# Lower-part score products over 128 rows instead of 64, in a two-block transformer kernel

## Chip, cores and metric

The kernel runs on one core of one Trainium2 chip. The metric is device time in microseconds (us) of one execution: the median of the runs shown. Engines in the profile: PE (TensorE matmul), PEld (its weight load), DVE (VectorE), ACT (ScalarE), POOL (GpSimd), SP (SyncE, which issues most DMAs).

## What is computed

Two transformer blocks of two layers each, on 256 tokens of width 1024, in f32. The first block mixes three attentions: a linear recurrence (RWKV-7), a dilated attention and a latent attention (MLA), each with 4 heads. The second mixes stick-breaking attention, a block-sparse one (which is plain causal at this length) and attention on a memory of 256 rows. Each layer of the first block ends with a gated feed-forward network. The scores that the change touches are these (cut):

```python
# latent attention: 128 columns "nope" and 64 rotated columns per head
s = (jnp.einsum('bqhd,bkhd->bhqk', qn, k_nope)
     + jnp.einsum('bqhd,bkd->bhqk', qr, k_rope)) * scale
# dilated, block-sparse and memory attention: heads of 64
s = jnp.einsum('...qhd,...khd->...hqk', q, k) * 64 ** -0.5
# recurrence, per head of 64, token after token
sa = jnp.einsum('bhvk,bhk->bhv', state, kk_t)
state = state * w_t - sa * b_t + v_t * k_t
y = jnp.einsum('bhvk,bhk->bhv', state, r_t)
```

The recurrence is computed in two halves of 128 tokens, in matrix form: its "scores" are products of (kk, r) with (b, k), masked to the past, and the inverse of a triangular matrix.

## The kernel before, in words

All operations are first recorded, in an order in which they could run one by one, by class `Plan` (line 208 on). `Plan.order` (430) then sorts them with a table of costs (`cost`, 303), gives each tile a place, and `issue` (546) emits the sorted list: every engine's order is fixed by it. A tile of fp32r type lies in an arena of `SPLIT` = 11264 columns (34), f32 tiles in another, and each waits for a free stretch of columns (`_find`, 338). `hold` (289) lets an operation wait for another one.

Matrices of weights come as pieces (`load`, 832): a DMA into `raw`, a cast to fp32r (`whi`, by ACT or DVE) and a subtraction for the rest (`wlo`, by DVE or POOL). `multiply` (863) makes three fp32r products per tile, upper with upper, upper with lower, lower with upper, all with 128 rows. This stream of weights goes on while attention runs, as far as the data allow.

Scores of heads of 64 that need the precision of f32 go through `stacked` (918). Two heads lie on the 128 partitions, one on 0 to 63 (q = 0), the other on 64 to 127 (q = 1). For each q, a tile `hi[q]` has the upper parts of that head on its own 64 partitions; on the other 64 it has, by a DMA of the POOL queue, the same again (queries, `twice`) or the lower parts (keys). So one product over 128 rows gives upper·upper + upper·lower. The third term, lower parts of the queries with upper parts of the keys, is a second product over the own 64 rows alone (`krl[rs]`, `dql[rs]`, `bql[rs]`, `ms["ql"][rs]`), into the same bank. Such pairs of products are in `rwkv` (1171, 8 pairs for each half of the tokens), `dilated` (1430, 4 pairs, second half alone), `moba` (1653, 6 pairs, second half alone) and `memory` (1669, 4 pairs per half): per layer 16 + 4 in the first block and 6 + 8 in the second, 68 in all.

In `mla` (1377) a head's scores are an f32 product over the 128 "nope" rows and an f32 product over 64 rotated rows, per block of 128 keys: 4 pairs for the first half of the tokens and 8 for the second, 24 in the two layers. An f32 product leaves two MATMUL records in the trace, an fp32r one leaves one.

Of the kernel before, what the change touches and what calls it, by code (L numbers as in the profile page):

```python
# [112 lines left out]
class View:  # L113
    """A slice of a tile that has no address yet: how to take it, and which part it covers."""
# [51 lines left out]
    @staticmethod  # L166
    def meet(r, q):
        """Whether two regions may share an element; a comb is (distance of its teeth, from, to)."""
        if r[0] > q[1] or q[0] > r[1] or r[2] > q[3] or q[2] > r[3]:
            return False  # L170
        a, b = r[4], q[4]
        return a is None or b is None or a[0] != b[0] or (a[1] < b[2] and b[1] < a[2])
# [8 lines left out]
class Tile(View):  # L181
    """ring: of how many slots, taken in turn, the tile takes one; 0: a place of its own in the arena."""
# [27 lines left out]
class Plan:  # L210
    """Takes the operations of the kernel in an order in which they could run one by one, gives
    the tiles their places, and issues the operations in an order in which no engine waits for
    one while it could run another."""
# [75 lines left out]
    def hold(self, o, d):  # L289
        """Let o, the last one recorded, wait for d."""  # L290
        if d is not None and d not in o.deps:
            o.deps[d] = True
            o.need += 1
            d.succ.append(o)
# [37 lines left out]
    def _kind(self, t):  # L332
        """Which arena the tile t lies in, and what it takes of it."""
# [4 lines left out]
    def _find(self, t, strict):  # L338
        """(time from which it is free, where) for the tile t, or None if it has to wait."""
# [73 lines left out]
    def flush(self, sizes, window):  # L413
        """Order and issue all that is recorded."""
# [15 lines left out]
    def order(self, sizes, window, strict, tiles):  # L430
# [23 lines left out]
        # the clock of TensorE is halved when less than a third of a window of 3.4 us was busy  # L454
# [113 lines left out]
class Piece:  # L568
    """A part of a weight matrix: ks k tiles of w columns, and its place among the k tiles of the activations."""
# [6 lines left out]
class Chunk:  # L576
    """Products of the activations lhs() with some columns of a weight matrix.

    rows: (bank, columns of a piece, how many) -> [token, column], for each half of the tokens
    cols: (bank, which half of it, first of 128 columns) -> [column, token], both halves at once  # L580
    """
# [9 lines left out]
def kernel(ctx: ExitStack, tc: tile.TileContext, ins, out):  # L591
# [66 lines left out]
    # cos and sin of the angles, both halves: [pos, 16 | pos, 64 | token index, 16]  # L658
# [31 lines left out]
    def rope(t, h, lo, n, heads):  # L690
        """Half-split rotation, in place, of t: [P, heads, 2, n]."""
# [9 lines left out]
    def rsqrt(v, n, most=None, soon=False):  # L701
        """1 / sqrt(v) of [P, n], v kept."""
# [38 lines left out]
    def rstd_of(src, soon=False):  # L741
        """1 / rms of the rows of src: [P, D]."""
# [9 lines left out]
    def across(r, dst):  # L752
        """The column r [P, 1] as a row dst [P, 128] on every partition."""
# [8 lines left out]
    def parts(n, tag):  # L762
        """Transposed activations of both halves, in two parts: [channel, half, k tile, token]."""
        return tuple(T([P, 2, n, P], tag + s, F32R) for s in ("h", "l"))

    def fill(dst, h, src, j, g):
        """Columns j*512..+512 of the rows src, transposed, times g [P, k tile], split."""
# [17 lines left out]
    def cut(loads, kts, w):  # L785
        """Pieces of at most two k tiles and 1024 columns in all."""
# [17 lines left out]
    def row_chunk(w, ca, cb, lhs, done, pre=None):  # L804
        """Columns ca..cb, as rows of tokens."""
# [3 lines left out]
    def col_chunk(w, spans, lhs, done, pre=None):  # L809
        """The columns of the spans, 128 to a block, as columns of tokens: done(block, [P, 256])."""  # L810
# [8 lines left out]
    def out_chunk(w, ks, banks, lhs, done, n):  # L819
        """Rows of a [K, 1024] matrix, one k tile to a piece: ks are (k tile of w, of the activations)."""  # L820
# [7 lines left out]
    def meanwhile(n, f):  # L828
        """Record f, loads above all, when n more pieces have come, to start when the last of them is split."""
        pending.append((count[0] + n, f))  # L830
# [32 lines left out]
    def multiply(h, chunk, pi):  # L863
        """The rows of half h of a piece, and with half 0 its columns."""
# [7 lines left out]
        def product(key, a, b, acc, pairs):  # L872
            """acc += of three products; the first in a bank clears it."""
# [29 lines left out]
    def run():  # L903
        """Record the stream: the second half of the tokens runs LAG pieces behind the first."""
# [13 lines left out]
    def stacked(dims, tag, twice, srcs):  # L918
        """srcs, (which part of [P, ...dims], what), heads of 64 by two, split for products over 64: [q]
        with the upper parts of the heads 2p + q on their own partitions, and on the other 64 the same  # L920
        again (twice) or the lower parts; and the lower parts of all."""
        hi = [T(dims, f"{tag}{q}", F32R) for q in range(2)]
        lo = T(dims, tag + "l", F32R)
        for part, src in srcs:
            for q in range(2):
                plan.either("copy", part(hi[q]), src)
            nc.vector.tensor_tensor(part(lo), src, part(hi[0]).bitcast(F32), op=OP.subtract)
        pat = "p a b c -> p (a b c)" if len(dims) == 4 else "p a b -> p (a b)"
        for q in range(2):
            own, other = slice(64 * q, 64 * q + 64), slice(64 - 64 * q, 128 - 64 * q)  # L930
# [22 lines left out]
    def flip(S, n, nkh):  # L953
        """[P q, n, nkh*128] -> [P keys, n, nkh, 128 q]."""
# [9 lines left out]
    def weigh(pts, vs, pairs, nkh):  # L964
        """Heads of 64, transposed, [2 x 64, pair, 128 q]: the values vs(kh, head) under the weights pts[head]."""
# [27 lines left out]
    # =====================  keys and values of the memory  =====================  # L993
# [841 lines left out]
```

## Time and profile before

| | us |
|---|---|
| median of the runs (1050.58, 1052.13, 1053.52) | 1052.13 |
| span of the profiled execution, first to last instruction | 1050.8 |
| PE busy in it | 1005.6 |
| DVE busy | 763.1 |
| ACT busy | 513.2 |
| POOL busy | 208.4 |

The profile is one execution. Busy time is a union: a matmul's record runs from its start to its modelled end, and the next one starts long before that, so PE looks busy even where matmuls follow slowly. How fast matmuls go is read from the distances between their starts. The granted TensorE clock is 1 (2.4 GHz) or 0.5 (1.2 GHz). All instructions have the same source line, so rows are told apart by operation, tile and shape; `128*128 128x256` is a matmul of 128 rows by 128 columns of weights with 256 moving columns.

### The profile page before, as it was taken

What the parts mean: (1) busy time and instruction counts of PE and PEld (TensorE: products, weight loads), DVE (VectorE), ACT (ScalarE), POOL (GpSimd) and SP (SyncE); (2) the same over time, 40 slices, a digit from 0 to 9 for tenths busy, and PEclk for the clock granted to TensorE, in tenths of its full rate; (3) what the DMA queues carried; (4) which work ended last, traced back from release to release, by engine and by line L of the source; (5) the groups of instructions that cost most, each with busy time, mean ns of one, the idle gap of its engine ahead of it and who ended that gap; (6) DMA issues with size and microseconds to landing.
All of it is one profiled execution on the core that took longest, in us unless ns stands there. A gap on an engine that the chain in (4) does not pass through costs nothing.

```text
span 1050.8 us, 20310 instructions
## 1 busy us (share of the span) xinstructions
PE 1005.6 (96%) x7473; PEld 889.7 (85%) x7473; DVE 763.1 (73%) x1796; ACT 513.2 (49%) x1232; POOL 208.4 (20%) x313
## 2 busy tenths in 40 slices
PE   7789999999999998999999999999989999999997
PEld 6677889799999987787777999999878988889886
DVE  6797667886676767976757876667687787766884
ACT  5475665443333344553543433333466466554673
POOL 3263021210100115351412101001132011220120
PEclk9999899999999999987979999999999999999999
DMA  6836115566565647552224565656454435465341
GB/s 208 250 100 214 45 53 162 156 184 200 170 207 170 197 118 217 145 145 82 70 73 141 181 210 166 210 169 200 126 136 131 142 111 186 137 157 146 111 161 41
DMA packets 108311, 158.39 MB, mean 151 GB/s; under 512 B 8433, under 2 KB 91571, under 8 KB 108211
## 3 DMA queue, kind: packets, MB, share of 16 engines
q1 hardware_dynamic: 105011, 151.97, 48.1%
q0 software_dynamic: 3200, 5.11, 2.2%
q8 instruction: 59, 0.97, 0.4%
q14 instruction: 41, 0.34, 0.1%
HBM read 148.74 MB, written 1.05 MB: 143 GB/s over the span
## 4 chain that ended last, share of the span: by engine, by line
PE 79%; DVE 13%; DMA 3%; issue 2%; ACT 2%; POOL 1%; SPq 0%; ACTq 0%; DVEq 0%; POOLq 0%
PE bank L565 79%; DVE plain L565 7%; DVE small L565 3%; DVE wlo L565 2%; DMA plain<-plain 1%; DVE split L565 1%; POOL small L565 1%; DMA raw<-in_w_in_dram 1%; ACT plain L565 1%; SPq L565 0%; DMA small<-in_positions_dram 0%; DVE whi L565 0%; DMA plain<-in_gains_dram 0%; ACT whi L565 0%; ACT plain L561 0%
## 5 line engine op out<-in xcount | busy, mean ns | idle before, releaser
L565 PE MATMUL bank<-whi,split 128*128 128x512 f32 (+4 forms) x1416 | 428.0, 371 | 4.1 <-DVE split L565 4.1
L565 ACT CAST whi<-raw 128x512 fp32r<-128x512 f32 (+4 forms) x412 | 219.2, 562 | 294.6 <-PE bank L565 217.1
L565 PE MATMUL bank<-split,whi 128*128 128x256 f32 x1904 | 353.9, 284 | 0.0
L565 DVE TENSOR_TENSOR wlo<-raw,whi 128x512 fp32r<-128x512 f32 (+4 forms) x489 | 296.4, 643 | 31.3 <-ACT whi L565 18.2
L565 PEld LDWEIGHTS bank<-split,whi 128*128 128x128 f32 x1904 | 299.8, 189 | 9.1 <-issue 2.3
L565 PEld LDWEIGHTS bank<-whi,split 128*128 128x128 f32 x1416 | 264.1, 193 | 36.5 <-DVE split L565 5.7
L565 PE MATMUL bank<-split,wlo 128*128 128x256 f32 x952 | 269.8, 283 | 0.0
L565 PE MATMUL bank<-wlo,split 128*128 128x512 f32 (+4 forms) x708 | 263.0, 372 | 2.7 <-DVE wlo L565 2.7
L565 POOL TENSOR_TENSOR wlo<-raw,whi 128x384 fp32r<-128x384 f32 (+3 forms) x107 | 131.4, 1241 | 656.8 <-DVE plain L565 235.5
L565 PE MATMUL bank<-plain 32*32 32x32 f32 (+7 forms) x2309 | 186.2, 251 | 24.3 <-DVE plain L565 9.3
L565 PEld LDWEIGHTS bank<-plain 32*32 32x32 f32 (+4 forms) x2309 | 141.8, 141 | 63.5 <-issue 20.5
L565 PEld LDWEIGHTS bank<-split,wlo 128*128 128x128 f32 x952 | 180.0, 189 | 1.2 <-issue 0.5
L565 DVE CAST whi<-raw 128x512 fp32r<-128x512 f32 (+4 forms) x184 | 72.6, 399 | 129.6 <-PE bank L565 114.0
L565 PEld LDWEIGHTS bank<-wlo,split 128*128 128x128 f32 x708 | 137.1, 194 | 18.1 <-DVE wlo L565 3.3
L565 ACT ACTIVATE plain<-plain 128x256 f32<-128x256 f32 (+4 forms) x155 | 71.7, 476 | 80.7 <-DVE plain L565 77.5
L565 DVE TENSOR_TENSOR plain<-bank,plain 128x256 f32<-128x256 f32 (+4 forms) x134 | 63.2, 492 | 29.7 <-PE bank L565 26.4
L565 ACT COPY plain<-bank 128x256 f32<-128x256 f32 (+6 forms) x129 | 50.3, 406 | 56.7 <-PE bank L565 55.2
L565 DVE TENSOR_TENSOR plain<-plain 128x256 f32<-128x256 f32 (+7 forms) x137 | 67.1, 505 | 6.9 <-DMA plain<-plain 2.8
L565 DVE TENSOR_TENSOR split<-plain,split 128x256 fp32r<-128x256 f32 (+2 forms) x94 | 61.8, 674 | 0.8 <-ACT split L565 0.3
L565 PE MATMUL bank<-split 128*128 128x256 f32 (+2 forms) x168 | 53.8, 377 | 0.0
L565 ACT CAST split<-plain 128x256 fp32r<-128x256 f32 (+2 forms) x100 | 47.6, 488 | 12.3 <-DVE plain L565 12.1
L565 POOL TENSOR_TENSOR small<-small 128x1 f32<-128x1 f32 (+2 forms) x98 | 28.0, 287 | 88.9 <-DVE small L565 68.5
(61 smaller groups left out, 521.9 us busy)
## 6 DMA issues: line engine op xcount, KB each, us to landing
raw<-in_w_in_dram SPq DMA_DIRECT2D x80, 384.0 KB, 3.5
raw<-in_ffn_w_gate_dram SPq DMA_DIRECT2D x88, 256.0 KB, 2.9
raw<-in_ffn_w_up_dram SPq DMA_DIRECT2D x88, 256.0 KB, 3.3
raw<-in_ffn_w_down_dram SPq DMA_DIRECT2D x44, 512.0 KB, 4.5
raw<-in_w_out_dram SPq DMA_DIRECT2D x32, 512.0 KB, 3.5
raw<-in_w_in_dram SPq DMA_DIRECT2D x24, 352.0 KB, 3.5
raw<-in_w_mem_kv_dram SPq DMA_DIRECT2D x8, 512.0 KB, 4.9
raw<-in_w_in_dram SPq DMA_DIRECT2D x16, 256.0 KB, 2.8
```

The source lines that it names most:

```text
L565: getattr(eng, name)(*args, **kw)
```

## The change

In `stacked` the lower parts of queries become two tiles `lo[q]`, one per q, which hold the head's lower parts on its own 64 partitions and zeros on the other 64. The second product of a pair then runs over all 128 rows. Per call with `twice` (10 in all: 4 in `rwkv`, 2 each in `dilated`, `moba`, `memory`) this is one tile more, two POOL memsets of 64 partitions (held until the source is written), and two DVE subtractions of 64 partitions in place of one of 128. In `mla` the transposed rotated queries go into two tiles with zeros likewise (two POOL memsets, two copies of 64x256 and one of 128x128 in place of one of 128x384), the rotated keys of both halves lie side by side, and one product takes both key blocks: in the second half 8 pairs with 128 columns become 4 pairs with 256. Docstrings and comments that the diff drops are left out here.

```diff
@@ stacked @@
         hi = [T(dims, f"{tag}{q}", F32R) for q in range(2)]
-        lo = T(dims, tag + "l", F32R)
+        pat = "p a b c -> p (a b c)" if len(dims) == 4 else "p a b -> p (a b)"
+        sides = [(slice(64 * q, 64 * q + 64), slice(64 - 64 * q, 128 - 64 * q)) for q in range(2)]
+        if twice:
+            begun = srcs[-1][1].tile.writes[-1][0]
+            lo = [T(dims, f"{tag}l{q}", F32R) for q in range(2)]
+            for q, (own, other) in enumerate(sides):
+                plan.hold(nc.gpsimd.memset(lo[q].rearrange(pat)[other, :].bitcast(F32), 0.0), begun)
+        else:
+            lo = T(dims, tag + "l", F32R)
         for part, src in srcs:
             for q in range(2):
                 plan.either("copy", part(hi[q]), src)
-            nc.vector.tensor_tensor(part(lo), src, part(hi[0]).bitcast(F32), op=OP.subtract)
-        pat = "p a b c -> p (a b c)" if len(dims) == 4 else "p a b -> p (a b)"
-        for q in range(2):
-            own, other = slice(64 * q, 64 * q + 64), slice(64 - 64 * q, 128 - 64 * q)
+            if twice:
+                for q, (own, other) in enumerate(sides):
+                    nc.vector.tensor_tensor(part(lo[q])[own], src[own], part(hi[q])[own].bitcast(F32), op=OP.subtract)
+            else:
+                nc.vector.tensor_tensor(part(lo), src, part(hi[0]).bitcast(F32), op=OP.subtract)
+        for q, (own, other) in enumerate(sides):
             nc.gpsimd.dma_start(hi[q].rearrange(pat)[other, :], (hi[q] if twice else lo).rearrange(pat)[own, :])
@@ rwkv @@
-                        nc.tensor.matmul(b[:, p * 256:(p + 1) * 256], bk[q][rs, p, j, :], krl[rs, p, :, :], start=False, stop=True, skip_group_check=True)
+                        nc.tensor.matmul(b[:, p * 256:(p + 1) * 256], bk[q][:, p, j, :], krl[q][:, p, :, :], start=False, stop=True, skip_group_check=True)
@@ mla @@
             rope(qr[h].rearrange("p a (b c) -> p a b c", b=2), h, 8, 32, 6)
+            begun = plan.ops[-1]
...
-            rT = lat["r", h] = T([P, 3, P], "qrT")
-            plan.either("copy", rT.rearrange("p a b -> p (a b)"), b[:, :384])
+            rT = [T([P, 2, P], f"qrT{q}") for q in range(2)]
+            for q in range(2):
+                own, other = slice(64 * q, 64 * q + 64), slice(64 - 64 * q, 128 - 64 * q)
+                plan.hold(nc.gpsimd.memset(rT[q].rearrange("p a b -> p (a b)")[other, :], 0.0), begun)
+                plan.either("copy", rT[q].rearrange("p a b -> p (a b)")[own, :], b[own, 0:256])
+            if h == 0:
+                lat["r"] = T([P, 256], "krT")
+            plan.either("copy", lat["r"][:, h * P:(h + 1) * P], b[:, 256:384])
...
-                    for kh in range(nkh):
-                        o = bv[:, p, kh * P:(kh + 1) * P]
-                        nc.tensor.matmul(o, lat["q"][:, hd, h * P:(h + 1) * P], lat["k"][:, hd, kh * P:(kh + 1) * P], start=True, stop=False)
-                        nc.tensor.matmul(o, rT[rs, p, :], lat["r", kh][rs, 2, :], start=False, stop=True)
+                    nc.tensor.matmul(bv[:, p, :], lat["q"][:, hd, h * P:(h + 1) * P], lat["k"][:, hd, 0:nk], start=True, stop=False)
+                    nc.tensor.matmul(bv[:, p, :], rT[q][:, p, :], lat["r"][:, 0:nk], start=False, stop=True)
@@ dilated (moba and memory alike) @@
-                nc.tensor.matmul(dst, dql[rs, p, :], dk[q][rs, p, :], start=False, stop=True, skip_group_check=True)
+                nc.tensor.matmul(dst, dql[q][:, p, :], dk[q][:, p, :], start=False, stop=True, skip_group_check=True)
```

## Rows read from the trace of the kernel before

**Rows 1.** Page, part 1: busy us, share of the span, instructions of each engine.
```profile
PE 1005.6 (96%) x7473; PEld 889.7 (85%) x7473; DVE 763.1 (73%) x1796; ACT 513.2 (49%) x1232; POOL 208.4 (20%) x313
```
**Rows 2.** Page, part 4: the chain that ended last, by engine.
```profile
PE 79%; DVE 13%; DMA 3%; issue 2%; ACT 2%; POOL 1%; SPq 0%; ACTq 0%; DVEq 0%; POOLq 0%
```
**Rows 3.** That chain in order of time: start us, us, engine, out, instructions.
```profile
88.21 3.14 DVE wlo L565 x4
...
92.05 73.03 PE bank L565 x950
...
474.27 22.67 PE bank L565 x378
...
795.85 104.60 PE bank L565 x739
...
934.40 106.64 PE bank L565 x760
```
**Rows 4.** Groups by form, whole span: count | busy us, mean ns | idle before.
```profile
L565 PE MATMUL bank<-split 64*128 64x256 f32 x68 | 27.1, 398 | 0.0
```
**Rows 5.** Timeline of PE, memory scores, second block: start us, us, instruction, count.
```profile
854.89 2.57 PE L565 MATMUL bank<-split 128*128 128x256 f32 x8
857.39 0.39 PE L565 MATMUL bank<-split,wlo 128*128 128x256 f32 x1
```
**Rows 6.** Timeline of PE, stream of weights, feed-forward network.
```profile
300.01 0.28 PE L565 MATMUL bank<-split,wlo 128*128 128x256 f32 x1
...
300.37 0.28 PE L565 MATMUL bank<-split,wlo 128*128 128x256 f32 x1
```
**Rows 7.** Timeline of PE, end of the first block's attention, layer 2.
```profile
520.03 3.23 PE L565 MATMUL bank<-plain 128*128 128x128 f32 x27
...
523.01 1.92 PE L565 MATMUL bank<-split 128*128 128x256 f32 x6
...
526.54 0.59 PE L565 MATMUL bank<-whi,split 128*128 128x512 f32 x1 [1.60 <-DVE split L565]
```
**Rows 8.** Groups by form, PE, 145.8 to 149.5 us: latent scores, layer 1.
```profile
L565 PE MATMUL bank<-plain 64*128 64x128 f32 x12 | 2.4, 322 | 0.0
L565 PE MATMUL bank<-plain 128*128 128x128 f32 x10 | 2.1, 311 | 0.0
```
**Rows 9.** Timeline of PE, latent scores, layer 2, second half.
```profile
533.22 4.97 PE L565 MATMUL bank<-plain 64*128 64x64 f32 x15
538.12 0.79 PE L565 MATMUL bank<-wlo,split 128*128 128x512 f32 x1
```
**Rows 10.** Stretches: length, busy us of PE, PEld, DVE, ACT, POOL, granted clock, DMA.
```profile
95.50:100.10 4.60, 4.60 (x61) 2.85 (x46) 2.81 (x11) 1.43 (x2) 2.11 (x12) 1.00 0.51 185
100.20:110.30 10.10, 10.10 (x111) 8.81 (x114) 5.76 (x19) 4.53 (x9) 1.57 (x8) 0.50 0.12 29
...
462.00:468.70 6.70, 6.70 (x24) 5.97 (x24) 4.25 (x13) 1.96 (x5) 0.82 (x1) 0.50 0.56 177
...
479.10:492.60 13.50, 13.50 (x195) 10.68 (x195) 6.27 (x29) 3.40 (x14) 0.00 (x0) 0.50 0.01 4
...
526.90:540.40 13.50, 13.50 (x46) 9.85 (x46) 6.77 (x36) 5.81 (x20) 0.31 (x2) 0.50 0.30 106
```
**Rows 11.** Timeline of PE, stream products inside the third of these stretches.
```profile
483.10 0.41 PE L565 MATMUL bank<-split,wlo 128*128 128x256 f32 x1
483.31 0.52 PE L565 MATMUL bank<-whi,split 128*128 128x384 f32 x1
```
**Rows 12.** Groups by form, whole span: what waits for the products, and the nearest costs.
```profile
L565 DVE COPY_PREDICATED plain<-plain,bank 128x512 f32<-128x512 int32 x16 | 11.7, 733 | 9.1 <-PE bank L565 9.0
...
L565 DVE TENSOR_TENSOR split<-bank,split 128x512 fp32r<-128x512 f32 x16 | 10.8, 686 | 3.1 <-ACT split L565 3.0
...
L565 POOL MEMSET plain<- 128x512 f32 x16 | 8.0, 547 | 1.6 <-DVE plain L565 1.6
...
L565 DVE TENSOR_TENSOR plain<-bank,plain 64x512 f32<-64x512 f32 x2 | 1.4, 695 | 1.6 <-PE bank L565 1.6
```

More of the change, by code (lines that the diff above doesn't have):

```diff
@@ L1165, in rwkv @@
                 for q in range(2):
-                    rs = slice(64 * q, 64 * q + 64)
                     plan.hold(nc.gpsimd.memset(dst[q].rearrange("p a b c -> p (a b c)"), 0.0), begun)
@@ L1387, in mla @@
             for q in range(2):
-                rs = slice(64 * q, 64 * q + 64)
                 b = bank()
@@ L1654, in scores @@
                 nc.tensor.matmul(dst, bq[q][:, p, :], bk[q][:, p, :], start=True, stop=False, skip_group_check=True)
-                nc.tensor.matmul(dst, bql[rs, p, :], bk[q][rs, p, :], start=False, stop=True, skip_group_check=True)
+                nc.tensor.matmul(dst, bql[q][:, p, :], bk[q][:, p, :], start=False, stop=True, skip_group_check=True)
             groups = [(0, [0, 1, 2]), (1, [0, 1, 2])] if h == 0 else [(0, [0, 1]), (1, [0, 1]), (0, [2]), (1, [2])]
@@ L1671, in scores @@
                 nc.tensor.matmul(dst, ms["q"][q][:, p, hs], ms["k"][q][:, p, :], start=True, stop=False, skip_group_check=True)
-                nc.tensor.matmul(dst, ms["ql"][rs, p, hs], ms["k"][q][rs, p, :], start=False, stop=True, skip_group_check=True)
+                nc.tensor.matmul(dst, ms["ql"][q][:, p, hs], ms["k"][q][:, p, :], start=False, stop=True, skip_group_check=True)
             o = softmax_heads(
```

## The prediction

> **What bounds the kernel now.** I read the page's busy shares first: PE is busy for 1005.6 of 1050.8 us, DVE for 763.1, the others for half the span or less [rows 1]. Then the chain that ended last: 79% of it is PE, 13% DVE [rows 2]. In order of time the chain shows where: in layer 1 PE alone from 92.05 us on for 73.03 us, in layer 2 for 22.67 us from 474.27, and in the second block two unbroken stretches of over 100 us [rows 3]. The products that the change touches lie in or just ahead of those stretches. What stands between is DVE, as at 88.21 us, where four `wlo` subtractions release PE [rows 3]. So PE's time counts nearly one for one where the chain stays on PE, and hardly where DVE comes next.
>
> A busy PE says little of its pace, so I then read starts. The 68 products of 64 rows have records of 398 ns [rows 4], but the record has the latency in it. In the memory scores four pairs, eight products of 256 columns with 128 and 64 rows in turn, go from 854.89 to 857.39: 2.50 us, or 0.31 us a product, 0.625 a pair [rows 5]. The stream of weights issues products of the same 256 columns, all of 128 rows, accumulating into one bank as well: three from 300.01 to 300.37, 0.12 us each (0.119 over the five threes from there) [rows 6]. The alternating pair pays 0.39 us over two products of one form. Nothing waits for data in between; idle before the 64-row products is 0.0 [rows 4].
>
> The Trainium skill's page "TensorEngine Tiling (Array Packing)", section Key Properties, says that changing the tiling mode drains the TensorE; the trace agrees with 0.31 us against 0.12. The same page speaks against the change as well: its section When to Use Tiling wants row tiling where 64 or fewer rows are contracted, since two such tiles work side by side. By that, 68 products given up as halves would cost 34 times 0.12, some 4 us (an estimate by that page); here no two of them stand next to each other, each lies between products of 128 rows, so I put nothing for it.
>
> **The change part by part.**
>
> *Split pairs.* 68 pairs [rows 4], each 0.625 us now [rows 5], after it two products of one form, 0.24 us [rows 6]: 68 times 0.39 is 26.3 us off PE. Six of these pairs run at half clock, where the saving is larger; that is in the bounds of the clock below.
>
> *Latent scores.* An f32 product of 128 columns is two records, and 27 such in one form take 520.03 to 523.01, 0.110 us each [rows 7]. In layer 1, from 145.8 to 149.5, 22 records (12 of them of 64 rows, six products) take 3.7 us, 0.168 each [rows 8]: 22 times 0.058 is 1.3 us for six products, 0.21 each. In layer 2, second half, 15 records go from 533.22 to 538.12, 0.327 us each [rows 9], at half clock [rows 10], where a one-form product of 256 columns takes 0.21 [rows 11]; I take the same for a record there. That is 15 times 0.117, 1.8 us for three and a half products, 0.5 each. So 16 products at 0.21 and 8 at 0.5: 7.4 us. Bounds: 5 (first-half products whose neighbours stay in other forms save half) to 9.4 (24 times 0.39). Eight of the second half's 16 products per layer go, since one takes 256 columns; the columns are the same, so I put nothing for it, and half the weight loads, which overlap PE.
>
> *The clock.* Four stretches of 10.1, 6.7, 13.5 and 13.5 us run at 1.2 GHz, 43.8 us in all [rows 10]. Just ahead of the first, from 95.5 to 100.1, PE ran the recurrence's alternating pairs at full clock, 61 instructions with PEld busy for 2.85 of 4.6 us [rows 10]; the last starts after 1.60 us of idle [rows 7]. With the alternation gone PE does the same work in less time, and the clock may stay up. Upper bound: some 18 us of the 43.8 are changed products (6 pairs at about 1.0, 8 latent ones at 1.4), the other 26 would take 0.12 / 0.21 of that, 11 us less, and the changed ones 4 less: 15. Lower bound: another 10 us stretch falls, minus 4. I take plus 4, nearer to none, because the small products of the triangular inverse between, which fill the third stretch (195 instructions [rows 10]), stay as they are.
>
> *What is not cashed.* (1) Three dilated pairs of layer 2 run from 523.01 on and are followed by 1.60 us in which PE waits for DVE [rows 7]: minus 1.2. (2) The first half's eight recurrence pairs in either layer are followed by a DVE stretch, as at 88.21 [rows 3]. DVE itself waits for those products, 9.0 us in 16 masked copies [rows 12], so it gains too; I count half of 2 times 3.1 as lost: minus 3, bounds 0 to 6.
>
> *What is added.* (3) DVE: a subtraction of 64 partitions costs as much as one of 128, 695 against 686 ns for 512 columns [rows 12]. Ten calls make one more: four of 512 columns, 2.8 us, and six of 256 to 512, about 0.6 each, 3.5 us. In `mla` three copies replace one, at most 0.7 us [rows 12] four times. Nine us in all, on an engine that is 73% busy [rows 1]. What hides it is PE's own stream; where DVE is on the chain it is not hidden. I charge a quarter, minus 2 (bounds 0 to 9). (4) POOL: 28 memsets at 0.55 or less [rows 12], 15 us on an engine busy for 208.4 [rows 1]. Behind them in POOL's queue stand the rsqrt steps, its `wlo` parts, and the DMA that duplicates `hi`, for which the first product of each pair waits: at most 1.1 us per call, 11 us in all. They may start when the source is transposed, while the two copies of `hi` are still to be made, which that DMA needs anyway: minus 1 (0 to 11). (5) Places: at the recurrence of layer 2 the fp32r arena must hold `hT` (4096 columns), `cT` (1536) and ten tiles of 512 for both halves, 10752 of 11264; with twelve it would be 11776, so tiles of the second half wait until the first half's go free. The second half's products come more than 10 us later, so the wait is short: minus 1 (0 to 5). Other orders that the planner makes from this I can't price.
>
> *Sum.* 26.3 + 7.4 + 4 - 1.2 - 3 - 2 - 1 - 1 = 29.5 us. Against the profiled execution: 1050.8 - 29.5 = 1021.3; nothing outside its span is shown. The median lies 1.3 above that span, so 1022.6; I say 1022.
>
> **Rivals.**
>
> *DVE takes PE's place.* Where PE is faster in the first block, it waits for `wlo`, masked copies and casts instead. For it: DVE 73% busy, the stretch at 88.21 [rows 1, 3], and more DVE work. Against it: 73 us of chain on PE alone in layer 1 [rows 3], and DVE itself waits for the pairs [rows 12]. Then the second block's 28 pairs remain, 10.9 us, and a third of the first block's 15.5 + 7.4, 7.6, less 4 for the additions: 14.5, time 1037 (1034 to 1046).
>
> *The clock stays up.* All four stretches run at full clock: 11 more than in the sum, 1011, and with less lost to DVE down to 1002. For it: the first fall follows the alternation directly [rows 10]. Against it: the last follows idle [rows 7], and small products remain. By the Trainium skill, page "TensorE: Matmul & The Clock Gate", Part 1, the throttled state is the default and activity releases it, which would make this case; the trace bears it out in part, as one of the two falls shown follows idle, not sparse work.
>
> *The change doesn't do what it says.* The 0.31 us could come from two products in a row into the same bank, or from the same weights loaded twice, and not from 64 rows. Then pairs stay at 0.625 and only the additions remain: 1052 to 1058. Against it: the stream accumulates into one bank at 0.12 [rows 6].
>
> *Slower: the freed time of PE becomes idle, and the clock falls.* The place is the first block's attention, above all 92 to 165, where PE has no idle now. At half clock a product takes 0.21 instead of 0.12 [rows 6, 11], so each us there loses 0.43. From 78 us more at half clock on (33.7 / 0.43) the gain is gone; with 100 it would be 43 - 29.5, some 1065. Against it: half clock is 44 us of the whole now, and long stretches of the stream hold full clock.
>
> **Chances and range.** Forecast, 1010 to 1034: 0.67. DVE takes over: 0.17. Clock stays up, 1002 to 1010: 0.08. Not what it says: 0.05. Slower by the clock: 0.03. About 0.3%, some 3 us, is what a measurement of this kernel can tell from no change. The first three cases are all faster by more: 0.92. Of the fourth, 0.03 falls within 0.3% and 0.02 above, with 0.03 of the fifth: slower 0.05. The range 1003 to 1042 leaves out the last two cases (0.08), the upper third of the DVE case (0.05) and tails of some 0.04.
>
> **What would show it.** After the change the page should have no 64*128 form with `bank<-split`, and 136 more evenly placed 128*128 128x256 ones: eight memory scores in about 1.0 us where [rows 5] has 2.50. If eight still take 2.5, the third rival holds. PE has 32 fewer records. POOL has 44 memsets, DVE ten more subtractions. If the chain's share of DVE rises from 13% to 16% or more, and PE's idle after DVE with it, the first rival holds; if the half-clock stretches of [rows 10] shrink to one or none, the second. The prediction is wrong if the spacing falls as said and the end does not move by 10 us or more, or if it moves by over 45.

## The result and the profile after

The changed kernel takes 1009.94 us (median of 4 runs, 1009.03 to 1014.56) against 1052.83 us before, measured beside it (4 runs, 1050.58 to 1057.67): a ratio of 0.960, 95% interval 0.957 to 0.963. The gain is 43 us, where the prediction has 30. The profiled execution's span is 1007.4 us; that of before is 1050.8. Experiments are named e1 to e12 below.

The page of the changed kernel, parts 1 and 4 (busy us, share of the span, instructions; then the chain by engine):

```profile
PE 959.0 (95%) x7441; PEld 864.6 (86%) x7441; DVE 767.9 (76%) x1806; ACT 516.7 (51%) x1240; POOL 220.1 (22%) x341
...
PE 75%; DVE 14%; DMA 4%; ACT 2%; issue 2%; POOL 1%; SPq 1%; DVEq 0%; ACTq 0%; POOLq 0%
```

Beside [rows 1, 2]: PE's busy time falls by 46.6 us, and the rest of the span, in which PE has no work on record, grows from 45.2 to 48.4, by 3.2. That makes the 43.4 us between the spans. So nearly all of the gain was kept, and PE is still the bound: DVE on the chain rose by one point only.

The groups by form of the changed kernel (count, busy us, mean ns, idle before and what ended it):

```profile
L565 PE MATMUL bank<-split 128*128 128x256 f32 x136 | 23.5, 303 | 1.4 <-DMA split<-split 1.0 <-DVE plain L565 0.3
...
L565 DVE COPY_PREDICATED plain<-plain,bank 128x512 f32<-128x512 int32 x16 | 11.1, 728 | 1.8 <-POOL wlo L565 1.2 <-PE bank L565 0.3
...
L565 POOL MEMSET split<- 64x512 f32 x12 | 6.2, 519 | 0.7 <-PE bank L565 0.2
...
L565 DVE TENSOR_TENSOR split<-bank,split 64x512 fp32r<-64x512 f32 x8 | 5.5, 686 | 0.9 <-ACT split L565 0.8
```

The form of [rows 4] is gone and there are 136 of one form. DVE no longer waits for them: its masked copies idled 9.0 us for PE [rows 12], now 0.3.

PE's timeline in the changed kernel: six split products of the recurrence in layer 1, then four memory scores, each with the instruction that follows (start us, us, instruction, count):

```profile
93.34 0.98 PE L565 MATMUL bank<-split 128*128 128x256 f32 x6
94.15 0.34 PE L565 MATMUL bank<-wlo,split 128*128 128x384 f32 x1
...
950.25 0.64 PE L565 MATMUL bank<-split 128*128 128x256 f32 x4
950.73 0.28 PE L565 MATMUL bank<-split,wlo 128*128 128x256 f32 x1
```

Four memory scores take 0.48 us, 0.12 each, where [rows 5] has 0.31. The first of these two groups answers to a row of before that the prediction did not show, at the same place:

```profile
95.54 1.95 PE L565 MATMUL bank<-split 128*128 128x256 f32 x6
97.42 0.45 PE L565 MATMUL bank<-plain 32*32 32x32 f32 x32
```

Six products until the next one starts: 1.88 us before, 0.81 after.

The stretches of [rows 10] in the changed kernel, where its own half clock lies nearby, too (length, busy us of PE, PEld, DVE, ACT, POOL, granted clock, DMA):

```profile
75.10:78.30 3.20, 3.20 (x14) 3.20 (x13) 1.86 (x8) 0.98 (x3) 2.85 (x7) 0.50 0.00 0
100.20:110.30 10.10, 9.82 (x195) 8.31 (x195) 7.75 (x36) 7.20 (x18) 6.08 (x22) 1.00 0.23 74
...
460.80:464.00 3.20, 3.20 (x73) 2.85 (x66) 2.36 (x9) 1.40 (x3) 1.75 (x2) 0.50 0.78 283
479.10:492.60 13.50, 13.50 (x253) 11.50 (x251) 7.32 (x25) 8.47 (x22) 3.54 (x12) 1.00 0.10 31
526.90:540.40 13.50, 11.13 (x52) 8.71 (x51) 10.74 (x22) 5.99 (x12) 6.31 (x5) 1.00 0.43 130
```

Three of the four stretches stand at 1.00 (2.4 GHz) instead of 0.50. Read in steps of 0.1 us, without the last 2 to 4 us of a span (at half clock in every kernel here), the clock is at half for 58.1 us before and for 20.4 after. Of the 43.8 us of [rows 10] 3.4 are left, from 460.7 on; two stretches of 3.4 us, from 75.0 and from 426.6 on, are new.

**Where the 46.6 us of PE's time went.** I took for each product the time from its start to the start of the next PE record. For the split products these sum to 42.2 us before (135 intervals) and 19.3 after (136): 22.9. For the latent products 20.9 (96 records) and 11.0 (64): 9.9. For all other products at half clock I took what each needs beyond the median interval of its form at full clock: 17.9 us before (378 products), 7.5 after (104): 10.4. That is 43.2; the other 3.4 I did not follow. The last of the three terms hangs on how it is worked out: with the median over products of the same tiles and shape, and no limit on what one product may have lost, it is 21.2 - 8.4 = 12.8, so the clock's part is 10 to 13 us and the unfollowed rest 1 to 3.

By place, from when the same product of the stream of weights starts in both traces: the first block of layer 1 gains 8.8 us, that of layer 2 23.2, the second block of both layers together 11.4. All four stretches of [rows 10] lie in the first block. The second block has 28 of the pairs, all at full clock before, and 28 times 0.39 is 10.9.

### The profile page after: what moved, and what is told of

It reads as the page before. It is cut to its first block, busy times and chain, and to the rows that moved or that the text cites. A ratio compares the mean times of both kernels' runs of the same rounds, so it can differ in the third digit from the quotient of the medians.

```text
span 1007.4 us, 20288 instructions
## 1 busy us (share of the span) xinstructions
PE 959.0 (95%) x7441; PEld 864.6 (86%) x7441; DVE 767.9 (76%) x1806; ACT 516.7 (51%) x1240; POOL 220.1 (22%) x341
## 4 chain that ended last, share of the span: by engine, by line
PE 75%; DVE 14%; DMA 4%; ACT 2%; issue 2%; POOL 1%; SPq 1%; DVEq 0%; ACTq 0%; POOLq 0%
PE bank L565 75%; DVE plain L565 7%; DVE small L565 3%; DVE split L565 2%; DVE wlo L565 2%; DMA plain<-plain 1%; ACT plain L565 1%; POOL small L565 1%; DMA plain<-in_c_dram 1%; SPq L565 1%; DMA raw<-in_w_in_dram 0%; DMA split<-split 0%; DMA small<-in_positions_dram 0%; ACT whi L565 0%; ACT split L565 0%
## 5 line engine op out<-in xcount | busy, mean ns | idle before, releaser
L565 DVE TENSOR_TENSOR wlo<-raw,whi 128x512 fp32r<-128x512 f32 (+4 forms) x489 | 302.8, 655 | 25.3 <-ACT whi L565 16.0
L565 POOL TENSOR_TENSOR wlo<-raw,whi 128x384 fp32r<-128x384 f32 (+4 forms) x107 | 129.5, 1222 | 609.9 <-DVE whi L565 263.4
L565 PE MATMUL bank<-plain 32*32 32x32 f32 (+8 forms) x2277 | 168.3, 242 | 26.7 <-DVE plain L565 9.9
L565 PEld LDWEIGHTS bank<-plain 32*32 32x32 f32 (+4 forms) x2277 | 128.5, 133 | 61.2 <-issue 15.4
L565 ACT ACTIVATE plain<-plain 128x256 f32<-128x256 f32 (+5 forms) x155 | 71.5, 476 | 77.7 <-DVE plain L565 71.6
L565 DVE TENSOR_TENSOR plain<-bank,plain 128x256 f32<-128x256 f32 (+4 forms) x134 | 63.2, 490 | 23.3 <-PE bank L565 21.2
L565 ACT COPY plain<-bank 128x512 f32<-128x512 f32 (+7 forms) x137 | 52.8, 399 | 42.4 <-PE bank L565 38.5
L565 DVE TENSOR_TENSOR plain<-plain 128x256 f32<-128x256 f32 (+7 forms) x137 | 63.0, 474 | 5.5 <-DMA plain<-plain 3.7
L565 DVE TENSOR_TENSOR split<-plain,split 128x256 fp32r<-128x256 f32 (+3 forms) x96 | 64.1, 681 | 0.4
L565 ACT ACTIVATE plain<-plain,small 128x128 f32<-128x128 f32 (+2 forms) x68 | 32.0, 475 | 13.4 <-DVE small L565 13.3
```

Of the source, the lines that this page charges most:

```text
L565: getattr(eng, name)(*args, **kw)
```

## The experiments

One table first. The last five columns are from each kernel's one profiled execution: PE's busy time, the rest of the span, the intervals of split and of latent products (blank where they were not read), and the time at half clock. Before was measured again beside each group of experiments, at 1053.5 us (e1, e2, e6, e7), 1053.9 (e3, e8, e9) and 1051.8 (e11, e12); their ratios are against these.

| kernel | median us | ratio to before, 95% | PE busy | rest | split | latent | half clock |
|---|---|---|---|---|---|---|---|
| before | 1052.8 | | 1005.6 | 45.2 | 42.2 | 20.9 | 58.1 |
| changed | 1009.9 | 0.957 to 0.963 | 959.0 | 48.4 | 19.3 | 11.0 | 20.4 |
| e7_rows_only | 1025.3 | 0.971 to 0.977 | 974.5 | 48.4 | 18.2 | 21.3 | 47.7 |
| e6_order_of_after | 1050.8 | 0.993 to 0.999 | 1004.1 | 44.9 | 43.5 | 14.7 | 71.6 |
| e1_split_only | 1022.3 | 0.969 to 0.976 | 963.5 | 57.2 | 20.0 | 18.2 | 20.6 |
| e2_latent_only | 1039.9 | 0.985 to 0.993 | 1003.0 | 41.7 | 44.6 | 11.6 | 64.8 |
| e3_recurrence_only | 1034.9 | 0.979 to 0.987 | 988.6 | 50.8 | 32.4 | 17.8 | 40.8 |
| e9_three_64 | 1032.2 | 0.974 to 0.982 | 980.6 | 49.7 | 22.4 | | 41.0 |
| e12_grouped | 1029.9 | 0.977 to 0.983 | 980.6 | 47.9 | 25.8 | | 44.3 |
| e11_halves_in_turn | 1024.3 | 0.972 to 0.977 | 965.9 | 52.6 | 21.2 | | 30.6 |
| e8_zeros_where_due | 1013.1 | 0.959 to 0.964 | 967.0 | 53.4 | 20.7 | 11.0 | 47.8 |

The profiled executions of e2, e3 and e8 are each the longest of their kernel (spans 1044.7, 1039.4 and 1020.4), at the lowest mean clock or next to it; that of e11 is the shortest (1018.5). For these the medians are the better measure of size.

**The disputed price by itself (e10_probe).** A row of products behind the last output of before:

```
+ groups = [(full, full)] * 120 + [(full, up)] * 100 + [(full, full)] * 120 + [(up, up)] * 200
+          + [(full, full)] * 120 + [(up, low)] * 200 + [(full, full)] * 120
+ for g in groups:
+     for rs in g:
+         nc.tensor.matmul((pr2 if rs is low else pr)[:, 0:256], pa[rs, 0:P], pb_[rs, :], start=True, stop=True)
```

> Before, and behind its last output a row of products of split tiles, 128 columns stationary by 256 moving, with nothing to wait for: 240 of 128 rows; 100 pairs of 128 and 64 rows; 240 of 128; 400 of 64 rows on the same half; 240 of 128; 200 pairs of 64 rows on the one half and the other; 240 of 128. It is the disputed price by itself. Theory 1: products of 128 rows every 0.12 us, the pairs of 128 and 64 rows every 0.45 to 0.65 us, 64 rows on the same half every 0.12 us, the clock at half in the pairs alone. Theory 2 (64 rows as such): 0.25 us or more for each product of 64 rows, and half clock there too. Theory 3 (the clock doesn't depend on the form, but on waits between the products): full clock in all of them, and pairs at about 0.4 us.

Measured in its one execution, as stretches of the probe (same columns as above): products of 128 rows; the first 3.2 us of the pairs; the pairs from there; 64 rows on one half; 64 rows on both halves in turn.

```profile
1060.00:1080.00 20.00, 20.00 (x169) 20.00 (x168) 0.00 (x0) 0.00 (x0) 0.00 (x0) 1.00 0.00 1
1083.20:1086.40 3.20, 3.20 (x12) 1.91 (x11) 0.00 (x0) 0.00 (x0) 0.00 (x0) 1.00 0.00 0
1090.00:1180.00 90.00, 90.00 (x178) 50.37 (x177) 0.00 (x0) 0.00 (x0) 0.00 (x0) 0.50 0.00 0
...
1215.00:1255.00 40.00, 40.00 (x336) 40.00 (x335) 0.00 (x0) 0.00 (x0) 0.00 (x0) 1.00 0.01 1
1290.00:1308.00 18.00, 18.00 (x306) 18.00 (x304) 0.00 (x0) 0.00 (x0) 0.00 (x0) 1.00 0.01 2
```

Per product: 20 / 169 = 0.118 us with 128 rows, 40 / 336 = 0.119 with 64 rows. So 64 rows as such cost no more than 128. In alternation at full clock 3.2 / 12 = 0.27, and soon the clock falls to 1.2 GHz and stays there as long as the alternation lasts: 90 / 178 = 0.51, a pair 1.01 us, more than four times two products of one form. PE is busy for all of these 90 us on record; its weight loads take 50 of them, against all the time in the other stretches. The record shows no idling that could have taken the clock here; what was there is the alternation. Whether it is the change of form itself or the slower pace of products that comes with it, the probe does not separate. Theory 1 holds, at a price above its range once the clock is down; 2 and 3 fall.

**Rows alone, in before's order (e7_rows_only).**

```
- bk[q][rs, p, j, :], krl[rs, p, :, :]
+ bk[q][:, p, j, :], krl[:, p, :, :]        (and likewise at the three other places)
```

> Before's instructions in before's order; only the second split product of each pair runs over 128 rows instead of 64, at all four places. [...] The latent scores are left as before. Theory 1 (leaving the form with 64 rows saves 68 x 0.39 = 26.3 us, and TensorE's clock stays up in the stretches of split products where it was at half): 1052.8 - 26.3 - about 10 = 1016 (1010 to 1021), with the half-clock stretches of the recurrence in layer 1 and of layer 2's first block gone. Theory 2 (what went beyond the 26.3 us in the changed kernel came from the new order that the planner makes, not from the rows): the order is before's here, so 1023 to 1030, and the half-clock stretches stay. Theory 3 (the zeros, the doubled subtractions and the tiles of the change cost several us): 1005 or less, below the changed kernel although the latent scores are not touched.

1025.3 us, 28 less than before. The split products save 24.0 us, the other products at half clock 3 to 4 (17.9 to 14.7, by the first of the two workings above). Of the four stretches of [rows 10] the first and the third are back at full clock and the second in part, but one of 17 us lies on the latent scores of layer 2, whose records run from 512 to 522 here:

```profile
100.20:110.30 10.10, 9.47 (x213) 7.68 (x202) 9.40 (x29) 8.38 (x19) 0.00 (x0) 1.00 0.20 56
462.00:468.70 6.70, 6.12 (x122) 5.43 (x123) 4.42 (x11) 1.57 (x4) 0.28 (x1) 0.75 0.52 183
479.10:492.60 13.50, 13.10 (x282) 10.87 (x282) 7.66 (x23) 6.61 (x18) 1.36 (x2) 1.00 0.25 81
511.50:528.40 16.90, 16.90 (x56) 12.44 (x57) 7.10 (x36) 6.01 (x21) 2.45 (x11) 0.50 0.25 86
```

The time lies in theory 2's range (1023 to 1030), above theory 1's; but the recurrence's stretches are gone, which is theory 1's sign, and nothing of the order is changed here: every engine's instructions come in before's order. So the switches are paid back in full by rows alone, and the recurrence's clock too; what is short of theory 1 is the stretch on the latent scores. That these must change for it to go is not shown: in e1 they alternate as well, at full clock. Theory 3 finds no support. No zeros are written here, so the other 64 rows add lower parts of one head times lower parts of the other head of the pair. In the recurrence that term is not small (perhaps because the heads' rows are scaled by their decays, which I did not try), so this kernel is read for its time alone; e8 keeps the zeros there.

**The changed kernel's order, 64 rows (e6_order_of_after).**

```
- bk[q][:, p, j, :], krl[q][:, p, :, :]      - rT[q][:, p, :], lat["r"][:, 0:nk]
+ bk[q][rs, p, j, :], krl[q][rs, p, :, :]    + rT[q][rs, p, :], lat["r"][rs, 0:nk]
```

> The changed kernel's instructions in the changed kernel's order (zeros, subtractions, merged latent scores and all), but the second product of each split pair and the second latent product read only their own 64 rows; the planner is told that they have 128, so that its order is the changed kernel's to the last instruction. Against the changed kernel only the rows differ. Theory 1 (rows: the switch of form, and the clock with it): the gain goes all but wholly, 1052.8 plus the price of what is added, less up to 5 for the latent products that are merged: 1047 to 1060, with half-clock stretches in the recurrence. Theory 2 (order): 13 to 17 us of the gain stay without the rows: 1034 to 1041. Theory 3 (the added work costs several us): 1058 to 1068.

1050.8 us. With the same instructions in the same order on every engine, 64 rows instead of 128 give back 41 of the 43 us: split intervals 43.5 us, half clock 71.6, among it these stretches (same columns):

```profile
103.70:110.30 6.60, 6.60 (x92) 5.69 (x96) 4.42 (x19) 2.27 (x7) 1.25 (x7) 0.50 0.25 94
134.40:147.80 13.40, 13.40 (x55) 11.27 (x55) 5.78 (x19) 5.87 (x18) 1.45 (x4) 0.50 0.23 69
482.50:499.40 16.90, 16.90 (x174) 12.46 (x174) 9.37 (x34) 4.19 (x16) 2.80 (x4) 0.50 0.30 96
```

The planner's new order explains nothing by itself (theory 2). This kernel is 2.7 us faster than the 1053.5 of before, while its latent products, of which eight a layer are merged away, save 6.2 us; so 3 to 4 us go elsewhere. The 13.5 us more at half clock can account for them, and nothing is left that must be the price of what is added. Its executions also give a price of the clock: over the nine from 1043.35 us (58 us at half, 2 x 0.028 x 1041.5) to 1052.80, the slope is 0.38 us of time per us at half clock. It is no constant: the 35 executions of before measured beside the experiments give 0.2, and it is a tie between two readings, not a trial.

**Each half of the change alone (e1_split_only, e2_latent_only).** e1 has the diff without its `mla`, e2 has its `mla` alone:

```
e1: + nc.tensor.matmul(b[:, p * 256:(p + 1) * 256], bk[q][:, p, j, :], krl[q][:, p, :, :], ...)
e2: + nc.tensor.matmul(bv[:, p, :], rT[q][:, p, :], lat["r"][:, 0:nk], start=False, stop=True)
```

> The change in the split score products alone, with zeros and second lower tiles; the latent scores as before. Theory 1: the latent part was worth the 7.4 us of its sum, so 1009.9 + 7.4 = 1017 (1014 to 1020). If the latent part hid beside other work it was worth 0 to 2: 1010 to 1012. If the clock stays up only with both parts in place, layer 2's first block gives back part of its 23 us: 1022 to 1030.

> The change in the latent scores alone (both key halves in one product, zeros beside the queries' rotated parts); the split products as before. Theory 1: 1052.8 - 7.4 = 1045 (1042 to 1048), half-clock stretches of the recurrence still there. If the latent part hid beside other work: 1051 to 1053. If the memsets and the copies in two halves delay the scores more than the products save: 1053 to 1057.

Split alone gains 31 us (1022.3), latent alone 13 to 14 (1039.9); together 44 to 45 against 43. The parts add up, and each expectation of mine for theory 1 was missed by 5 us in the same direction: the latent part is worth 12 to 14, not 7.4. By its time e1 also lies at the edge of the third case (1022 to 1030), but not by its mechanism: its clock is up as in the changed kernel, with the latent scores as before. Between e1 and the changed kernel its products save 18.2 - 11.0 = 7.2 us, all at full clock, close to the 7.4 of the sum, and half clock is the same (20.6 and 20.4 us); and yet the two spans differ by 13.3 us: 4.5 in PE's busy time, 8.8 in the rest of the span, 57.2 in e1 and 48.4 in the changed kernel. PE's waits in e1 (us in total, times, longest):

```profile
PE bank L565 <- DVE plain L565: 16.7, 18, 2.3
```

In the changed kernel:

```profile
PE bank L565 <- DVE plain L565: 10.2, 13, 2.5
```

Why PE waits less for DVE with the merged products I did not try. In part it can be the planner's order: e8 and e11 have the merged products too, and 53.4 and 52.6 us in the rest. In e2 the recurrence's half clock stays, and the last stretch of [rows 10] is gone:

```profile
98.70:112.20 13.50, 13.50 (x137) 10.92 (x138) 7.52 (x25) 5.21 (x10) 2.90 (x14) 0.50 0.11 38
...
477.60:497.90 20.30, 20.30 (x272) 15.07 (x273) 10.36 (x38) 4.82 (x17) 2.22 (x2) 0.50 0.11 41
526.90:540.40 13.50, 12.95 (x79) 10.09 (x78) 12.66 (x40) 9.76 (x29) 5.78 (x12) 1.00 0.35 114
```

**The recurrence alone (e3_recurrence_only).**

```
- nc.tensor.matmul(b[:, p * 256:(p + 1) * 256], bk[q][rs, p, j, :], krl[rs, p, :, :], ...)
+ nc.tensor.matmul(b[:, p * 256:(p + 1) * 256], bk[q][:, p, j, :], krl[q][:, p, :, :], ...)
```

> The change in the recurrence's split products alone (32 of the 68 pairs, zeros included); dilated, block, memory and latent scores as before. Theory 1 (recurrence carries the half-clock stretches: 32 x 0.39 = 12.5 us of switches, less 4 for what is added, and some 30 us of half clock at 0.43 us each, the slope between executions of one kernel): 1053.5 - 12.5 + 4 - 13 = 1032 (1027 to 1037). Theory 2 (the gain of the split part, 31 us, goes evenly by pairs, and the clock is the same matter everywhere): 1053.5 - 31 x 32 / 68 = 1039 (1037 to 1043). If the clock in the first block is set by the latent and dilated scores as well, half-clock stretches stay at 100 to 110 and 479 to 493.

1034.9 us, 18 to 19 gained by 32 of the 68 pairs. That is in theory 1's range, but the four executions go from 1030.5 to 1041.6, so theory 2 is not ruled out by time. The split products account for 9.8 of the gain; layer 2's stretch at 479.1 to 492.6 is at 1.00, while 13.4 and 6.6 us at half clock now lie in layer 1, from 127.7 and from 155.0 on, right behind latent scores (123 to 129 us, 147 to 152) and dilated ones (153 to 155) that still alternate. Those of layer 2 alternate too, from 521.8 to 531.0, and no half clock follows.

**Half the switches, the same rows (e12_grouped).**

```
- for p: product of 128 rows (p); product of 64 rows (p)
+ for p: product of 128 rows (p)
+ for p: product of 64 rows (p)
```

> Before's products with before's rows, in another order within a bank: first the products of 128 rows of two or more pairs, then their products of 64 rows, so that the form changes about half as often (by the planner's list mostly 2 and 2, in places 4 and 4, where before has 1 and 1). Nothing is added, no row count is changed, the latent scores are as before. Theory 1 (each change of form costs, and many of them close together bring the clock down): about half of what the run with rows alone gained, 28 us: 1053.5 - 14 = 1039 (1033 to 1045). Theory 2 (the second products cost by their 64 rows, or by what waits around them): 1050 to 1056.

1029.9 us: 22 gained without one row more, more than theory 1 had. In the trace the form changes 71 times next to a split product, before it does so 144 times. A second sum is begun in a bank here before the first is complete, and the scores are not those of before, so this kernel is read for its time alone. Its groups by form, against 398 ns in [rows 4]:

```profile
L565 PE MATMUL bank<-split 64*128 64x256 f32 x68 | 15.8, 334 | 0.0
L565 PE MATMUL bank<-split 128*128 128x256 f32 x68 | 15.2, 307 | 0.0
```

The intervals fall from 42.2 to 25.8 us, by 16.4, more than half of e7's 24.0. So it is the switch that costs, not the rows.

**64 rows throughout (e9_three_64, e11_halves_in_turn).** Three products of 64 rows instead of one of 128 and one of 64; in e11 with the changed `mla`, and with the halves taken in turn:

```
- matmul(dst, dq[q][:, p, :], dk[q][:, p, :]);  matmul(dst, dql[rs, p, :], dk[q][rs, p, :])
+ matmul(dst, dq[rs, p, :], dk[rs, p, :]);  matmul(dst, dq[rs, p, :], dkl[rs, p, :]);  matmul(dst, dql[rs, p, :], dk[rs, p, :])
```

> The split scores of before as three products of 64 rows each (upper by upper, upper by lower, lower by upper) instead of one of 128 and one of 64; the copies and DMAs that stack the halves are gone; the latent scores as before. Theory 1 (the switch between the two forms costs, not the 64 rows): three at 0.12 us against the pair's 0.625 us are 0.36 us, 68 x 0.26 = 18 us gained, switches only at the ends of a group (about 40 groups x 0.2 = 8 us back), clock as in the run with rows alone: 1030 to 1043. Theory 2 (64 rows are slow as such, 0.3 us or more each): 68 x (0.9 - 0.625) = 19 us lost: 1066 to 1076. Where the clock falls in the recurrence here too though nothing alternates inside a group, it is the 64 rows that lower it, not the switching.

> Three products of 64 rows for each split score, without the stacking copies and DMAs, and the products of the two halves in turn, into two banks (in the probe such products came every 0.06 us, those of one half every 0.12); the latent scores as in the changed kernel. Against the changed kernel: 68 x (0.24 - 0.18) = 4 us less of products, the copies, zeros and DMAs of stacking gone (up to 5), some 20 groups x 2 changes of form x 0.2 = 8 us back: 1009 (1002 to 1016). If the entries and exits of the groups bring the clock down as alternating pairs do: 1016 to 1026. Against the run with three products of 64 rows of one half after the other (1032.2): 13 for the latent scores and about 12 for the halves in turn make 1007.

e9 takes 1032.2 us, within theory 1: half as many products again, yet 21 to 22 us less than before. Its recurrence runs at full clock:

```profile
100.20:110.30 10.10, 10.10 (x248) 8.37 (x246) 5.18 (x17) 5.23 (x17) 1.28 (x1) 1.00 0.64 212
...
479.10:492.60 13.50, 13.50 (x253) 11.18 (x251) 8.54 (x32) 8.57 (x28) 3.15 (x10) 1.00 0.05 18
```

So 64 rows do not lower the clock either. e11 takes 1024.3 us, 8 better than e9 where the latent part alone should give 12, and above the 1009 expected. Its 204 products take 21.2 us, 0.10 each, where the probe has 0.06. The Trainium skill, page "TensorEngine Tiling (Array Packing)", section Key Properties, says that different tiles can execute in parallel; the probe agrees (18 / 306 = 0.059 us a product with the halves in turn). In e11 the same pace is there inside a group. One group of 20:

```profile
72.61 1.46 PE L565 MATMUL bank<-split 64*128 64x256 f32 x20 [0.91 <-DVE split L565]
74.00 0.44 PE L565 MATMUL bank<-wlo,split 128*128 128x384 f32 x1
```

Of its 1.39 us the first and the last two products take 0.22 and 0.21, the 16 between them 0.95, which is 0.06 each. Over the whole kernel 151 of the 204 intervals, those under 0.15 us, sum to 9.0 us, 0.06 each; the other 53, at the ends of groups and beside other work, to 12.2, 0.23 each. So it is the ends of the groups that eat the gain of the halves in turn. e9 had part of that gain already: 59 of its 204 products start within 0.05 us of the one before. Against the changed kernel e11's split products cost 1.9 us more, its half clock is 10 us longer and the rest of its span 4 us, so its time lies in the second case of its expectation (1016 to 1026).

**Fewer additions (e8_zeros_where_due).** Zeros in the recurrence only; at the other three split places the product of e7; and in `mla`:

```
- nc.tensor.matmul(bv[:, p, :], rT[q][:, p, :], lat["r"][:, 0:nk], ...)
+ nc.tensor.matmul(bv[:, p, :], rT[:, p, :], lat["r"][q][:, 0:nk], ...)
```

> The changed kernel with fewer additions: zeros and second lower tiles only in the recurrence; in the dilated, block and memory scores the second product simply runs over 128 rows of what is there (the other half adds lower parts times lower parts of the other head); in the latent scores the zeros stand beside the keys, written once a layer, instead of beside the queries, written for each half. If the additions cost several us at the same clock (the runs so far suggest 4 to 6 for all of them): 1004 to 1008. If they lie beside other work: 1009 to 1012, as the changed kernel. If the order that the planner makes here brings TensorE to half clock for some 20 us more, as in the run with rows alone: 1012 to 1020.

1013.1 us, ratio 0.959 to 0.964 against 0.957 to 0.963 for the changed kernel: not to be told apart. Fewer additions gain nothing, so what the change adds is hidden as far as this can show, and no version here beats it. The profiled execution shows 23.7 us at half clock from 98.5 on, the third case of the expectation, and its span, 1020.4, is above the median.

## Why the prediction was right or wrong

**The bound and the split pairs: right.** PE's time counted nearly one for one, and 26.3 us were taken for the 68 pairs where the intervals give 22.9 (24.0 in e7). It is a little less because the products after the change also stand next to other forms now and then: 0.134 us a product at full clock on average (16.7 us over 125), not 0.118.

**The latent scores: the mechanism right, the size too small.** 7.4 was taken (5 to 9.4); their intervals fell by 9.9, and by themselves they are worth 12 to 14 us. The prices of 0.21 and 0.5 us came from averages in which other products stand. Of the 22 records of [rows 8] six belong elsewhere: four of 64 rows that follow each other in twos, 0.007 us apart, and two of 128 rows beside their like. Eight records that are latent products alone, from 146.94 to 148.61, take 0.21 us each, against 0.110 in one form: a pair of products is four records, so it pays 0.39 us, and 24 pairs 9.5, about the upper bound of the prediction. In [rows 9] three of the 15 records have 64 columns and are no latent scores either; the twelve that are go from 533.78 to 538.12, 0.36 us each and not 0.327 (groups by form from 533.78 to 538.10: count | busy us, mean ns | idle before):

```profile
L565 PE MATMUL bank<-plain 128*128 128x128 f32 x6 | 2.4, 500 | 0.0
L565 PE MATMUL bank<-plain 64*128 64x128 f32 x6 | 2.4, 498 | 0.0
```

The working covered the products alone. The half clock of layer 2's second half was in it for the changed products only; their neighbours' part, and the waits of PE that shrink with them (e1), were not.

**The clock: the term that was mis-sized.** Plus 4 was taken out of minus 4 to 15. Outside the changed products alone it gave 10.4 us (up to 13 by the other working), and a part within them. The step that failed is the choice inside the bounds. It rested on the small products of the triangular inverse, which "stay as they are": they did, and their stretch of [rows 10] holds 1.00 all the same. And it took the idle of [rows 7] as evidence that the last fall had another cause. Where the alternating products of before lie speaks against that: the recurrence's from 95.5 to 101.7, 457.7 to 463.6 and 474.7 to 480.6 us, latent and dilated ones from 510 to 524, and the four stretches of [rows 10] begin at 100.2, 462.0 and 479.1, with three products of each recurrence group still to come, and at 526.9, right after PE's wait of 1.60 us [rows 7]. The probe then showed the alternation by itself at half clock with no idle time of PE on record. But alternation alone does not settle where the clock falls. Before has 16 alternating products of the recurrence from 78.05 to 83.81 and 56 in the second block, and no stretch at half clock follows them; in e1 and e3 layer 2's latent scores still alternate, and the last stretch is at full clock there, in e7 it is not. What decides between these I leave open. So the rival "the clock stays up", with a chance of 0.08, is what happened but for one piece of 3.4 us, and the 1011 us worked out for it are the time that was measured, 1009.94, inside the range and just past the end of the likeliest case. That the two agree so closely is in part luck: 1011 has the clock at 11 us more than the forecast, and of the 14 us that were missing only 6 to 9 are the clock. The Trainium skill, page "TensorE: Matmul & The Clock Gate", Part 1, says that activity releases the throttle; the probe's row has PE busy on record for 90 of 90 us at 0.50, so a profile's busy share does not tell which level is granted.

**What was charged against it: too much.** Minus 8.2 in all for the pairs ahead of DVE's stretches, DVE's and POOL's new work and the places. The rest of the span grew by 3.2 us. DVE's busy time rose by 4.8 us of the 9 bounded, POOL's by 11.7 of 15, and the idle time ahead of DVE's masked copies fell from 9.1 to 1.8 us. Something like one of the charges shows: in layer 1 the first split product waits for the duplicating DMA, once, for 1.0 us. But no memset held it up, since POOL sat idle for 1.87 us before it issued the DMAs at 88.24. That such losses can come shows e1, where the rest grew by 12 us.

**The rivals.** DVE as the new bound fell: its share of the chain went from 13 to 14%, not 16. "Not what it says" fell with the 0.12 us spacing. The slower one fell: half clock shrank by 38 us.

In one line, 22.9 + 9.9 + 10.4 + 3.4 - 3.2 = 43.4 us, against 29.5: of the 14 us between, 6 to 9 are the clock, 2 to 3 the latent products and 5 the charges; split pairs took 3 off, and 1 to 3 stay unassigned.

## What to carry to other kernels

Read the pace of products from start to start, and by form: where two forms alternate, change the order or pad the smaller one to the larger, before cutting any work. Padding with zeros cost nothing that could be seen here, beside a busy PE. And price the clock by the stretches that follow an alternation, not only by the alternating products themselves.

## What the runs showed of the hardware

- Products with 128 and 64 rows in turn come every 0.27 us at full clock and every 0.51 at half, against 0.118 and 0.119 for either form alone, and TensorE's clock was at 1.2 GHz in the whole of the stretch shown (1090 to 1180 us), though the record has no idle time of PE in it; in the products of one form that followed (1215 to 1255 us) it was at 2.4 GHz (probe, one execution).
- In the kernel most alternating split products still ran at full clock themselves (124 of the 136 before); the half clock lay on the last of them and on what came after. Not every alternating group is followed by it: none of the second block is.
- Products of 64 rows on the two halves in turn, in two banks, came every 0.059 us in the probe, twice as often as on one half, and every 0.06 inside the groups of e11; the ends of those groups cost 0.23 us an interval.
- Between executions of one kernel, a microsecond at half clock went with 0.38 us of time in e6 (nine executions) and with 0.2 in before (35).
